# A decoder layer on eight cores: first Q tiles over six PSUM banks, earlier loads and norms of group B, LayerNorm 1 in tile order, and a rebalanced tail

## The chip, the cores and the metric

The kernel runs on all eight cores of one Trainium2 chip, as two dies of four cores (cores 0 to 3 and 4 to 7). Each core computes 2048 of the 16384 token positions. The time is the device time of the slowest core, in microseconds (us). Most executions agree within a few us (the fast ones of the kernel before took 3064.58 to 3069.06); some fall into a slower state in which one die, or both, show a lower granted TensorE clock (one of 3357.17 us had 0.90 on die 1 and 0.99 on die 0), and those are left out. Verdicts use fast executions alone, and less than 2% counts as "same".

The engines are named as the profile names them: PE is TensorE, PEld its weight loads, DVE VectorE, ACT ScalarE, POOL GpSimd, SP SyncE (which here only issues DMAs). In the lines of the profile `arena` is the one SBUF tensor that the program cuts into buffers, and `sp` its PSUM banks.

## The reference, cut to what matters

```python
D_MODEL = 2048; SEQ = 16384; D_FF = 5632
def token_mixer(x, ...):
    proj = x @ w_in + b_in
    # group A: 8 heads of 128, causal attention over three dilations (1, 4, 16), mixed
    ya = dilated_mixture_attention(qa, ka, va)
    # group B: 16 query heads of 64, 2 key/value heads, sliding window 128, with sinks
    yb = sink_window_attention(qb, kb, vb, sinks)
    y = concatenate([rms_norm(ya, g_mix_a), rms_norm(yb, g_mix_b)], -1)
    return y @ w_out
def reference(x, ...):
    x = layer_norm(ALPHA * x + token_mixer(x), ln1_g, ln1_b)      # LN1
    return layer_norm(ALPHA * x + swiglu(x), ln2_g, ln2_b)        # LN2
```

Matmuls run on bf16 operands and sum in f32.

## The kernel before: the parts that matter

A core passes through seven stages: the V projections, the first Q tiles, the attention of group B and then of group A (32 "units" each, with the remaining Q projections mixed in), the output projection (with LN1), the feed-forward part, and a tail that finishes LN2. The token block is handled in two halves of 1024, `st` = 0 and 1, from the output projection on. A helper records each operation with the buffers that it reads and writes, and the semaphores follow from that.

The first Q tiles. Each tile takes 16 matmuls into one PSUM bank, and the banks alternate between 6 and 7:

```python
def proj(tau, half=None):
    ...
    bk = 6 + tau % 2
    ...
LEAD = 6
for tau in range(LEAD):
    proj(tau)
    if tau:
        run(peq, 1)
pend = b_S(0, 0)            # first scores of group B
```

The sums for group B's RMS norm end in a small tensor, rb. It goes to DRAM from a scratch buffer `ls`, which ACT needs again in the next unit:

```python
S_.act(... out=ls, in_=ls, func=AF.Exp, scale=-0.5 ...)
S_.dma("act", k.rb_d[...], ls, [bls], [b], ...)
```

`ys` is y, the attention output, in DRAM. In unit 26 of group A SP issues the loads of rb and of 28 of the 32 pieces of y, for both halves; SP works through them in order (on core 4 these 32 issues went from 917.15 to 957.48 us, and the store of y behind them was issued at 957.58). `out_norm` multiplies one 128x512 piece of y by its norm on DVE, in place:

```python
for t in range(4):
    S_.dma("sp", k.rs[t][0], k.rb_d[...], ...)
for c in KCB:                # group B's pieces
    y_load(0, c)
for c in KCA[:6]:            # group A's pieces, without the last two heads
    y_load(0, c)
for c in KCB + KCA[:6]:
    y_load(1, c)
```

The output projection. A step takes one tile (n, hh): columns n of the model, half hh of the tokens. The tile z = ALPHA * x + projection is formed by DVE from the PSUM bank and from `xres`, a 256 KB load of x. POOL and ACT add up its statistics, and `finish` sums them over partitions with two matmuls:

```python
OUT_BK = (6, 7, 0, 1, 2, 3)
for si, (n, hh) in enumerate(steps):
    bk = OUT_BK[si % 6]
    load_xr(si + 3)                         # xres of a later tile, issued by SP
    ...
    out_mm(k, st, n, hh, bk, KCB + KCA, True, True)
    ...
    z, bz = slot("z%d_%d" % (st, si), o_h + (zbase[st] + si) * 2048)   # zbase = [12, 0]
    S_.dve(... z = ALPHA * xb + bank(k, bk) ...)
    ...                                     # statistics on ACT and POOL
    for _ in range(2 if si % 2 else 1):
        if jobs and not fins:
            jobs.pop(0)()                   # LN1 tiles of the other half
...
for hh in range(2):                         # LN1 tiles of this half become jobs
    for n in range(KC):
        jobs.append(... ln1_tile(st, n, hh, z, bz))
```

`ln1_tile` normalises z in place (two DVE operations), writes x1 in bf16 for the next matmuls and stores z to DRAM (`x1s`). Only when that store has landed is the slot of z free. The slots are tight: with `zbase` 12 and 0, z tile `si` of the second half takes the slot of z tile `si - 12` of the first. The last four tiles of the second half (`si` 28 to 31) load their xres into slots of z tiles 28 to 31 of the first half, because the ring of xres buffers has by then been given to the weights of the feed-forward part:

```python
if st == 1 and si >= 28:
    xr.append(slot("xrz%d" % si, o_h + (si + 12) * 2048))
```

The softmax here doesn't subtract the row's maximum and nothing guards it: scores larger than these inputs give would overflow.

Of the kernel before, what the change touches and what calls it, by code (L numbers as in the profile page):

```python
# [44 lines left out]
class Sched:  # L45
# [83 lines left out]
    def emit(self, final_wait_ops):  # L129
# [60 lines left out]
        for i in final_wait_ops:  # L190
            op = self.ops[i]
            last[op.semkey] = max(last.get(op.semkey, 0), op.val)
# [92 lines left out]
def persist(k):  # L285
# [14 lines left out]
    k.p_end = P.o  # L300
    for v, d in ((k.bqk, k.bqk_d), (k.bsw, k.bsw_d), (k.gmix, k.gmix_d), (k.lnp, k.lnp_d), (k.esink, k.sinks_d)):
        S_.dma("sp", v, d, [], [], "small", joins=[bs])
# [51 lines left out]
def phase1(k):  # L354
# [49 lines left out]
    o_r = XO + 4 * X_SLOT  # L404
    bvr, bbvr = view(k, o_r, VW, F32)[0:1], S_.buf("bvr", o_r, o_r + VW * 4)
    S_.dma("sp", bvr, k.bv_d[0][0:1], [], [bbvr], "bvr")
# [190 lines left out]
def phase2(k):  # L597
# [122 lines left out]
    def proj(tau, half=None):  # L720
# [10 lines left out]
        bk = 6 + tau % 2  # L731
# [236 lines left out]
    def reduce_b(t):  # L968
        bk = 6 + nx("pj", 2)
        S_.pe(lambda: nc.tensor.matmul(bank(k, bk), k.onesf, acc[:, t * 512:(t + 1) * 512], start=True, stop=True),  # L970
              [bacc[t], k.bonesf], [k.bBK[bk]])
        ls, bls = LS[nx("ls", 2)]
        S_.act(lambda: nc.scalar.activation(out=ls, in_=bank(k, bk), func=AF.Ln, bias=1024.0 * RMS_EPS, scale=1.0), [k.bBK[bk]], [bls])
        S_.act(lambda: nc.scalar.activation(out=ls, in_=ls, func=AF.Exp, scale=-0.5), [bls], [bls])
        b = Buf("rb%d" % t)
        S_.dma("act", k.rb_d[:, t * 512:(t + 1) * 512], ls, [bls], [b], "rbs%d" % t)
        rsum.append(b)

    LEAD = 6
    for tau in range(LEAD):  # L980
        proj(tau)
        if tau:
            run(peq, 1)
    pend = b_S(0, 0)
# [16 lines left out]
    for u in range(32):  # L1001
        h, c = u // 4, u % 4
        if c == 0 and h < 7:
            load_kv(h + 1)
        if u == 26:
            k.o_w, k.o_rs = o_w, o_ra
            run(dveq, 9)
            out_open(k, rsum)
        if u == 28:
            k.y_load(0, 6)  # L1010
            k.y_load(1, 6)
            wfill(k)
        for p_ in range(3):
# [11 lines left out]
            if u >= 28:  # L1025
                out_norm(k, *k.norms.pop(0))
# [8 lines left out]
    for i, (n, hh) in enumerate(OUT_PRE):  # L1035
        if i == 0:
            while len(k.norms) > 48:
                out_norm(k, *k.norms.pop(0))
# [4 lines left out]

KCB, KCA = list(range(8, 16)), list(range(8))
# [7 lines left out]
def out_open(k, rsum):  # L1052
# [16 lines left out]
    for t in range(4):  # L1069
        S_.dma("sp", k.rs[t][0], k.rb_d[:, t * 512:(t + 1) * 512], [rsum[t]], [k.rs[t][1]], "rs")  # L1070
    for c in KCB:
        y_load(0, c)
    for c in KCA[:6]:
        y_load(0, c)
    for c in KCB + KCA[:6]:
        y_load(1, c)
# [13 lines left out]
    k.wlive, k.wts = [("xr", 20480, W_RING)], {}  # L1090

# [44 lines left out]
def phase3(k):  # L1136
# [53 lines left out]
    def ln1_tile(st, n, hh, z, bz):  # L1190

        (mu, bmu), (rs, brs) = stat[hh]
        if st == 0:
            for bk, (v, b) in ((4, stat[hh][0]), (5, stat[hh][1])):
                if n == 0:
                    S_.act(lambda bk=bk, v=v: nc.scalar.activation(out=bank(k, bk), in_=v, func=AF.Copy), [b], [k.bBK[bk]])
            mu, rs, bmu, brs = bank(k, 4), bank(k, 5), k.bBK[4], k.bBK[5]
# [22 lines left out]
    for st in range(2):  # L1220
# [22 lines left out]
        for si, (n, hh) in enumerate(steps):  # L1243
            bk = OUT_BK[si % 6]
            load_xr(si + 3)
            xb, bxb = xrs[si]
            if st == 0 and si < 6:
                out_mm(k, st, n, hh, bk, KCA, False, True)
# [4 lines left out]
            for _ in range(2):  # L1253
                if st == 0 and k.norms:
# [18 lines left out]
        b0 = 4 if st == 0 else 6  # L1273
        fins += [lambda b0=b0: finish(0, b0), lambda b0=b0: finish(1, b0)]
        open_x1b(st)
        for hh in range(2):
            for n in range(KC):
# [29 lines left out]
    def finish_last(zl, bzl):  # L1307
# [18 lines left out]
        on_pool = (1, 4, 7, 10, 12, 14)  # L1326
# [15 lines left out]
        for n in range(KC):  # L1342
# [5 lines left out]
    for st in range(2):  # L1348
# [37 lines left out]
        for si, (n, hh) in enumerate(steps):  # L1386
# [34 lines left out]
            if jobs:  # L1421
                jobs.pop(0)()
# [117 lines left out]
```

## Time and profile before

| | before |
|---|---|
| fast runs, first measurement | 3064.58 and 3069.06 us |
| slow run | 3301.43 us |
| profiled execution | 3068.1 us, core 4 slowest; other cores 3050.9 to 3061.2 |

The page of the profile gives the span and the busy time of each engine (us, share of the span, number of instructions):

```profile
span 3068.1 us, 39918 instructions; the slowest of 8 cores (3050.9 to 3068.1 us)
PE 2964.0 (97%) x15721; PEld 1425.1 (46%) x15999; DVE 1057.6 (34%) x1440; ACT 656.0 (21%) x906; POOL 631.5 (21%) x593
```

PE bounds the kernel: busy 97% of the span, and 99.5% of the feed-forward part (1215 to 3034 us). PE's waits on core 4 of the kernel before (waiting line, what it waited for, us in total, times, longest):

```profile
PE sp L1130 <- DVE arena L1119: 11.2, 2, 10.7
PE sp L420 <- DMA arena<-bv: 10.3, 1, 10.3
PE sp L896 <- DVE arena L927: 8.8, 13, 3.5
...
PE sp L1130 <- DVE arena L1261: 5.8, 1, 5.8
PE sp L736 <- DVE arena L349: 3.9, 4, 1.1
PE sp L1366 <- DVE arena L1261: 3.7, 1, 3.7
PE sp L776 <- ACT arena L783: 2.2, 1, 2.2
PE sp L1366 <- DMA arena<-wup: 1.6, 1, 1.6
```

L1130 is the output projection, L1119 the norm of y, L1261 the forming of z, L736 a Q projection, L776 the first scores of B, L1366 the first feed-forward matmul ("up").

The chain of work that ended last, on core 4, shows what stands behind three of them (start, us, what):

```profile
957.58 11.89 DMA ys<-arena
969.52 3.82 DMA arena<-ys
974.11 0.76 DVE arena L1119
975.00 12.83 PE sp L1130 x48
...
1136.90 21.43 DMA x1s<-arena
1158.56 0.69 DVE arena L1261
...
1180.71 26.12 DMA x1s<-arena
1206.96 4.17 DMA arena<-xres
```

The last piece of y is stored at 957.6, read back, normalised, and only then can PE go on at 975.0. In the middle of the second half, at 1158.6, z waits for a slot whose x1s store took 21 us; at the end an xres load waits for a store of 26 us.

The timeline of PE on core 4 shows the first Q tiles and the first scores (start, us, engine, line, operation, count, idle time before and what ended it):

```profile
503.06 3.61 PE L736 MATMUL sp<-arena 128*128 128x512 bf16 x16 [0.95 <-DVE arena L349]
...
524.06 0.62 PE L776 MATMUL sp<-arena 64*128 64x256 bf16 x10 [2.18 <-ACT arena L783]
```

With two banks, each tile from the third on waits about 1 us until DVE has emptied the bank of the last but one.

### The profile page before, as it was taken

The numbers are of one execution on the slowest core, as the hardware profiler recorded it, in microseconds if no ns is written. First come the engines' busy times: TensorE is split into PE (matmuls) and PEld (weight loads), VectorE is DVE, ScalarE is ACT, GpSimd is POOL, SyncE is SP. The second block draws the span as 40 slices with busy tenths as digits, with TensorE's granted clock in tenths as the row PEclk, the third lists the DMA queues.
The fourth block names the chain that finished last, engine by engine and source line by source line (L and its number), as shares of the span: only waits on it lengthen the run. The fifth ranks groups of instructions, "written<-read, shape, count | busy, mean of one in ns | idle before, by whom it ended". The sixth has DMA issues, their size and how long they took to land.

```text
span 3068.1 us, 39918 instructions; the slowest of 8 cores (3050.9 to 3068.1 us)
## 1 busy us (share of the span) xinstructions
PE 2964.0 (97%) x15721; PEld 1425.1 (46%) x15999; DVE 1057.6 (34%) x1440; ACT 656.0 (21%) x906; POOL 631.5 (21%) x593
## 2 busy tenths in 40 slices
PE   8999999999997998999999999999999999999996
PEld 3445554545664443444444444444444444444442
DVE  1646545887787653430000100000322000000124
ACT  0000001765654133320000001111222000011123
POOL 2000000553444965000000002222000000002234
PEclk9999999999999999999999999999999999999998
DMA  9961213255657898564444348899676444435565
GB/s 165 180 142 61 87 44 75 46 124 134 134 130 192 172 185 178 130 130 77 79 73 83 69 99 205 207 205 203 140 153 135 83 76 75 81 102 178 185 206 168
DMA packets 192956, 397.92 MB, mean 130 GB/s; under 512 B 88961, under 2 KB 106625, under 8 KB 171778
## 3 DMA queue, kind: packets, MB, share of 16 engines
q0 software_dynamic: 31296, 167.06, 32.9%
q1 hardware_dynamic: 144770, 197.86, 21.9%
q10 hardware_dynamic: 16704, 30.42, 2.8%
q8 instruction: 129, 2.11, 0.3%
q14 instruction: 57, 0.47, 0.1%
HBM read 470.52 MB, written 91.82 MB: 183 GB/s over the span
## 4 chain that ended last, share of the span: by engine, by line
PE 91%; DMA 3%; ACT 2%; DVE 1%; SPq 1%; issue 1%; POOL 0%; DVEq 0%; ACTq 0%; POOLq 0%
PE sp L1366 39%; PE sp L1399 20%; PE sp L486 7%; PE sp L473 6%; PE sp L736 5%; PE sp L1130 5%; DMA x1s<-arena 2%; SPq L127 1%; PE sp L536 1%; PE sp L554 1%; PE sp L907 1%; DVE arena L927 1%; PE sp L795 1%; ACT arena L925 1%; PE sp L896 0%
## 5 line engine op out<-in xcount | busy, mean ns | idle before, releaser
L1366 PE MATMUL sp<-arena 128*128 128x512 bf16 x5519 | 1212.1, 379 | 11.2 <-DVE arena L1261 3.7
L1366 PEld LDWEIGHTS sp<-arena 128*128 128x128 bf16 x5632 | 551.3, 98 | 672.7 <-issue 10.6
L1399 PE MATMUL sp<-arena 128*128 128x512 bf16 x2760 | 605.3, 379 | 2.9
L1374 DVE TENSOR_TENSOR arena<-sp,arena 128x512 bf16<-128x512 f32 x176 | 121.8, 692 | 993.7 <-ACT arena L1373 993.7
L1399 PEld LDWEIGHTS sp<-arena 128*128 128x128 bf16 x2816 | 275.5, 98 | 332.6 <-issue 0.6
L1373 ACT ACTIVATE arena<-sp 128x512 f32<-128x512 f32 x176 | 105.1, 597 | 900.5 <-PE sp L1366 900.0
L127 POOL DMA_DIRECT2D arena<-wup x88 | 46.8, 532 | 1079.6 <-PE sp L1366 1063.1
L1170 POOL TENSOR_TENSOR arena<-arena 128x512 f32<-128x512 f32 x119 | 157.5, 1324 | 447.9 <-DVE arena L1410 393.5
L1130 PE MATMUL sp<-arena 128*128 128x512 bf16 x1003 | 225.3, 384 | 18.2 <-DVE arena L1119 11.2
L736 PE MATMUL sp<-arena 128*128 128x512 bf16 x979 | 229.9, 380 | 7.7 <-DVE arena L349 3.9
L1410 DVE SCALAR_TENSOR_TENSOR arena<-arena,sp 128x512 f32<-128x512 f32 x64 | 44.0, 688 | 520.8 <-ACT arena L1394 350.5
L486 PE MATMUL sp<-arena 128*128 128x512 bf16 x1001 | 220.1, 379 | 1.2
L473 PE MATMUL sp<-arena 128*128 128x384 bf16 (+1 forms) x1036 | 182.4, 337 | 0.4
L1130 PEld LDWEIGHTS sp<-arena 128*128 128x128 bf16 x1024 | 100.9, 99 | 143.3 <-issue 26.6
L1171 POOL TENSOR_TENSOR arena<-arena 128x512 f32<-128x512 f32 x119 | 160.3, 1347 | 1.1 <-ACT arena L1169 1.1
L486 PEld LDWEIGHTS sp<-arena 128*128 128x128 bf16 x1024 | 100.2, 98 | 120.3
L736 PEld LDWEIGHTS sp<-arena 128*128 128x128 bf16 x1024 | 96.8, 98 | 114.4 <-issue 9.2
L699 DVE TENSOR_TENSOR arena<-arena 128x1024 bf16<-128x1024 bf16 x160 | 141.3, 897 | 23.6 <-ACT arena L783 12.6
L473 PEld LDWEIGHTS sp<-arena 128*128 128x128 bf16 x1040 | 101.7, 98 | 79.6
L1394 ACT ACTIVATE arena<-arena 128x512 f32<-128x512 f32 x64 | 52.0, 813 | 394.9 <-DMA arena<-x1s 393.9
L343 ACT ACTIVATE arena<-sp,arena 128x512 bf16<-128x512 f32 (+1 forms) x37 | 25.1, 678 | 505.3 <-PE sp L510 383.1
L1169 ACT ACTIVATE arena<-arena 128x512 f32<-128x512 f32 x119 | 74.9, 630 | 201.6 <-DVE arena L1261 71.2
(130 smaller groups left out, 2062.2 us busy)
## 6 DMA issues: line engine op xcount, KB each, us to landing
arena<-wup POOLq DMA_DIRECT2D x88, 1024.0 KB, 8.2
arena<-wdb SPq DMA_DIRECT2D x32, 1408.0 KB, 7.7
arena<-wdn POOLq DMA_DIRECT2D x16, 1408.0 KB, 12.9
wdb<-arena SPq DMA_DIRECT2D x16, 1408.0 KB, 13.5
arena<-wout POOLq DMA_DIRECT2D x32, 512.0 KB, 10.7
arena<-xres SPq DMA_DIRECT2D x64, 256.0 KB, 8.6
x1s<-arena ACTq DMA_DIRECT2D x64, 256.0 KB, 8.1
arena<-x1s SPq DMA_DIRECT2D x64, 256.0 KB, 7.8
```

What stands on the lines that cost most here:

```text
L127: return self._add(q, lambda: eng.dma_start(out=out, in_=in_), reads, writes, joins, semkey=semkey)
L473: ins = nc.tensor.matmul(bank(k, bk)[:, 0:c1 - c0], x[:, kc, blk * 128:blk * 128 + 128], wv[:, kc, c0:c1], start=(kc == 0), stop=(kc == KC ...
L486: ins = nc.tensor.matmul(bank(k, bk), wk[h][:, kc, :], x[:, kc, :], start=(kc == 0), stop=(kc == KC - 1))
L699: S_.dve(lambda: nc.vector.tensor_tensor(out=pg, in0=pg, in1=m.to_broadcast([128, rows, 1024 // rows]), op=ALU.mult), [bp, b], [bp])
L736: ins = nc.tensor.matmul(bank(k, bk), w[:, kc, :], x[:, kc, :], start=(kc == 0), stop=(kc == KC - 1))
L1130: ins = nc.tensor.matmul(bank(k, bk), w[:, kc, :], y[:, kc, hh * 512:(hh + 1) * 512], start=(first and i == 0), stop=(last and i == len(kc ...
L1170: S_.pool(lambda: nc.gpsimd.tensor_tensor(out=za, in0=za, in1=z, op=ALU.add), [bz, bza], [bza])
L1171: S_.pool(lambda: nc.gpsimd.tensor_tensor(out=qa, in0=qa, in1=sq, op=ALU.add), [bsq, bqa], [bqa])
L1366: ins = nc.tensor.matmul(bank(k, a + half), w[:, kc, half * 128:half * 128 + 128], xb[:, kc, hh * 512:(hh + 1) * 512], start=(kc == 0), st ...
L1373: S_.act(lambda si=si, a=a: nc.scalar.activation(out=sg[si][0], in_=bank(k, a), func=AF.Silu), [k.bBK[a]], [sg[si][1]])
L1374: S_.dve(lambda si=si, a=a, f=f, hh=hh: nc.vector.tensor_tensor(out=h[f][:, hh * 512:(hh + 1) * 512], in0=bank(k, a + 1), in1=sg[si][0], o ...
L1399: ins = nc.tensor.matmul(bank(k, bk), w[:, fc, :], h[fc][:, hh * 512:(hh + 1) * 512], start=(fc == 0), stop=(fc == FC - 1))
```

## The change

The change means to take each of these waits away: six banks for the first Q tiles and the scores before the sixth tile; rb stored from the accumulator and not from `ls`; group B's y loaded in unit 24 and normalised in units 25 to 27, with the y of the second half moved into the output projection; the LN1 tiles in the order (n, hh) in which the slots are needed again, with mean and deviation of both halves in four banks; and the LN2 jobs of the tail dealt out anew between DVE and POOL. The core of the diff:

```diff
-        bk = 6 + tau % 2
+        bk = 6 + tau % 2 if tau >= 4 else (0, 1, 4, 5)[tau]
...
-        S_.dma("act", k.rb_d[:, t * 512:(t + 1) * 512], ls, [bls], [b], "rbs%d" % t)
+        S_.dma("act", k.rb_d[:, t * 512:(t + 1) * 512], at, [bacc[t]], [b], "rbs%d" % t)
...
     for tau in range(LEAD):
+        if tau == LEAD - 1:
+            pend = b_S(0, 0)
         proj(tau)
...
+        if u == 24:
+            k.o_w, k.o_rs = o_w, o_ra
+            out_open(k)                       # loads y of group B, first half (8 loads)
         if c == 0 and h < 7:
             load_kv(h + 1)
         if u == 26:
-            out_open(k, rsum)
+            for i in KCA[:6]:
+                k.y_load(0, i)
...
+            if u == 24 and p_ == 2:
+                rs_load(k, rsum)              # rb loads, now on ACT's queue
-            if u >= 28:
+            if (u, p_) in NORM_AT:            # 2, 3, 3 norms in units 25-27, 2 each in 28-31
                 out_norm(k, *k.norms.pop(0))
...
-            for bk, (v, b) in ((4, stat[hh][0]), (5, stat[hh][1])):
+            i = 4 + 2 * hh
+            for bk, (v, b) in ((i, stat[hh][0]), (i + 1, stat[hh][1])):
...
-            bk = OUT_BK[si % 6]
+            bk = OUT_BK[si % 6] if st == 0 else si % 4
             load_xr(si + 3)
+            if st == 0 and si < 8:
+                for c in (KCB + KCA[:7])[2 * si:2 * si + 2]:
+                    k.y_load(1, c)            # 15 loads of the second half's y
             if st == 0 and si < 6:
-                out_mm(k, st, n, hh, bk, KCA, False, True)
+                for c in KCA:
+                    out_mm(k, st, n, hh, bk, [c], False, c == 7)
...
-        for hh in range(2):
-            for n in range(KC):
+        for n in range(KC):
+            for hh in range(2):
                 jobs.append(... ln1_tile ...)
...
-        on_pool = (1, 4, 7, 10, 12, 14)
+        on_pool = (1, 4, 7, 10, 13)
...
-            if jobs:
-                jobs.pop(0)()
+            for _ in range(1 + st):
+                if jobs:
+                    jobs.pop(0)()
```

Smaller edits are cut: the bias bv is loaded first, the norms of the second half wait until step 8 of the output projection, and the last stores and their final waits come in another order.

More of the change, by code (lines that the diff above doesn't have):

```diff
@@ L189, in emit @@
         last = {}
-        for i in final_wait_ops:
+        for i in sorted(final_wait_ops):
             op = self.ops[i]
-            last[op.semkey] = max(last.get(op.semkey, 0), op.val)
+            last[op.semkey] = max(last.pop(op.semkey, 0), op.val)
         for key, val in last.items():
@@ L300, in persist @@
     k.p_end = P.o
+    o_r = XO + 4 * X_SLOT
+    k.bvr = (view(k, o_r, VW, F32)[0:1], S_.buf("bvr", o_r, o_r + VW * 4))
+    S_.dma("sp", k.bvr[0], k.bv_d[0][0:1], [], [k.bvr[1]], "bvr")
     for v, d in ((k.bqk, k.bqk_d), (k.bsw, k.bsw_d), (k.gmix, k.gmix_d), (k.lnp, k.lnp_d), (k.esink, k.sinks_d)):
@@ L402, in load_x @@
         bx[t] = bl
-    o_r = XO + 4 * X_SLOT
-    bvr, bbvr = view(k, o_r, VW, F32)[0:1], S_.buf("bvr", o_r, o_r + VW * 4)
-    S_.dma("sp", bvr, k.bv_d[0][0:1], [], [bbvr], "bvr")
+    bvr, bbvr = k.bvr
     s0 = xs[slot_of[0]]
@@ L973, in reduce_b @@
         S_.act(lambda: nc.scalar.activation(out=ls, in_=bank(k, bk), func=AF.Ln, bias=1024.0 * RMS_EPS, scale=1.0), [k.bBK[bk]], [bls])
-        S_.act(lambda: nc.scalar.activation(out=ls, in_=ls, func=AF.Exp, scale=-0.5), [bls], [bls])
+        at = acc[:, t * 512:(t + 1) * 512]
+        S_.act(lambda: nc.scalar.activation(out=at, in_=ls, func=AF.Exp, scale=-0.5), [bls], [bacc[t]])
         b = Buf("rb%d" % t)
-        S_.dma("act", k.rb_d[:, t * 512:(t + 1) * 512], ls, [bls], [b], "rbs%d" % t)
+        S_.dma("act", k.rb_d[:, t * 512:(t + 1) * 512], at, [bacc[t]], [b], "rbs%d" % t)
         rsum.append(b)
@@ L983, in phase2 @@
             run(peq, 1)
-    pend = b_S(0, 0)
     for u in range(32):
@@ L1005, in phase2 @@
         if u == 26:
-            k.o_w, k.o_rs = o_w, o_ra
             run(dveq, 9)
-            out_open(k, rsum)
+            for i in KCA[:6]:
+                k.y_load(0, i)
         if u == 28:
             k.y_load(0, 6)
-            k.y_load(1, 6)
             wfill(k)
@@ L1035, in phase2 @@
     for i, (n, hh) in enumerate(OUT_PRE):
-        if i == 0:
-            while len(k.norms) > 48:
-                out_norm(k, *k.norms.pop(0))
         out_mm(k, 0, n, hh, OUT_BK[i], KCB, True, False)
@@ L1041, in phase2 @@
             reduce_a(i + 1)
+NORM_AT = [(u, p) for u, ps in ((25, (1, 2)), (26, (0, 1, 2)), (27, (0, 1, 2)), (28, (0, 2)), (29, (0, 2)), (30, (0, 2)), (31, (0, 2)))
+           for p in ps]
 KCB, KCA = list(range(8, 16)), list(range(8))
@@ L1049, with out_open @@
 W_RING = 24576
-def out_open(k, rsum):
+def out_open(k):
     S_ = k.S
@@ L1068, in y_load @@
         S_.dma("sp", k.y[st][:, c, :], k.ys_d[c, :, st * TS:(st + 1) * TS], [k.bys[c]], k.by[st][c], "y")
-    for t in range(4):
-        S_.dma("sp", k.rs[t][0], k.rb_d[:, t * 512:(t + 1) * 512], [rsum[t]], [k.rs[t][1]], "rs")
     for c in KCB:
         y_load(0, c)
-    for c in KCA[:6]:
-        y_load(0, c)
-    for c in KCB + KCA[:6]:
-        y_load(1, c)
     k.y_load = y_load
@@ L1090, in out_open, with rs_load @@
     k.wlive, k.wts = [("xr", 20480, W_RING)], {}
+def rs_load(k, rsum):
+    for t in range(4):
+        k.S.dma("act", k.rs[t][0], k.rb_d[:, t * 512:(t + 1) * 512], [rsum[t]], [k.rs[t][1]], "rs")
 def wfill(k):
@@ L1193, in ln1_tile @@
         if st == 0:
-            for bk, (v, b) in ((4, stat[hh][0]), (5, stat[hh][1])):
+            i = 4 + 2 * hh
+            for bk, (v, b) in ((i, stat[hh][0]), (i + 1, stat[hh][1])):
                 if n == 0:
                     S_.act(lambda bk=bk, v=v: nc.scalar.activation(out=bank(k, bk), in_=v, func=AF.Copy), [b], [k.bBK[bk]])
-            mu, rs, bmu, brs = bank(k, 4), bank(k, 5), k.bBK[4], k.bBK[5]
+            mu, rs, bmu, brs = bank(k, i), bank(k, i + 1), k.bBK[i], k.bBK[i + 1]
         S_.dve(lambda: nc.vector.tensor_tensor(out=z, in0=z, in1=mu, op=ALU.subtract), [bz, bmu], [bz])
@@ L1253, in phase3 @@
             for _ in range(2):
-                if st == 0 and k.norms:
+                if st == 0 and si >= 8 and k.norms:
                     out_norm(k, *k.norms.pop(0))
@@ L1272, in phase3 @@
             jobs.pop(0)()
-        b0 = 4 if st == 0 else 6
-        fins += [lambda b0=b0: finish(0, b0), lambda b0=b0: finish(1, b0)]
+        fins += [(lambda hh=hh, b0=(4 + 2 * hh if st == 0 else 6): finish(hh, b0)) for hh in range(2)]
         open_x1b(st)
-        for hh in range(2):
-            for n in range(KC):
+        for n in range(KC):
+            for hh in range(2):
                 z, bz = zz[(n, hh)]
@@ L1341, in finish_last @@
             S_.pool(lambda z=z: nc.gpsimd.tensor_tensor(out=z, in0=z, in1=rs, op=ALU.mult), [bz, brs], [bz])
-        for n in range(KC):
+        for n in [0, 2, 1, 3, 5, 4, 6, 8, 9, 7, 11, 12, 10, 14, 15, 13]:
             ln2_out(n, TS + 512, *zr[(1, n, 1)], "sp")
```

## The prediction

> **What bounds it.** TensorE. The busy table has PE at 97% (2964 of 3068.1 us); in the windows of the feed-forward stages (1215 to 3034 us) it is 99.5%. What can be won is in about 104 us of PE idle time and in the half-rate matmuls after long idles. PE's waits (core 4) and the timeline show where:
>
> - start: 10.3 us for the DMA of bv, 0.9 for ACT;
> - first Q tiles, 495-527 us: four waits of 1 us (projection waits for DVE to empty bank 6/7), 2.2 (scores wait for exp), 0.4, then six matmuls at 0.43 instead of 0.216 us;
> - 712.8 us: 3.5 us, ACT held by the DMA store of rb from its scratch buffer;
> - 975 us: 10.65 us. The chain of waits runs through the ys store issued at 957.6 and its reload at 969.5; the store stood on the SP queue behind 28 y loads that took 35 us to issue. Then 11 matmuls at 0.43 us: 2.3 us more. [...];
> - 1153 us: 5.8 us (PSUM bank <- DVE <- a slot whose x1s store took 21 us), plus 2.3 slow;
> - 1200-1212 us: 1.6 + 3.7 us: the last out-projection tiles wait for xres behind a 26 us x1s store;
> - tail: last down matmul 3038.7, end 3068.1; POOL's sixth tile ends at 3061.4, a leftover tile is stored at 3063.7.
>
> **The change, costed.**
> 1. bv first: ACT still waits for the small loads (10.5 us) and its table load; other cores wait for wv: 1 us.
> 2. Six banks, scores before the sixth tile: 3.9 + 2.6 + 1.3 slow = 8 us, all on PE's chain.
> 3. rb stored from acc: 2-3 us.
> 4. B's y at unit 24, the second half's y moved to the out projection, rb loads on ACT's queue: removes 10.65 + 2.3 + 0.6. Adds four norms (0.75 us or more of DVE) in units 25-27, takes one each from 28-31: zero net. Per-chunk waits on 16 norms at 0.68 us cost 1-1.5. The 8 y loads (2 MB at some 200 GB/s: 10 us) delay head 7's K/V: 0-3 us risk. Net 10-12 on core 4, 6-9 on the others, whose wait was 5.6-8.4.
> 5. Tile order: the 1153 stall goes (8 us on core 4, 0-3.5 elsewhere). The end of that stage stays or gets a few us worse: DMA share is 1.0, and the first up tile now needs the banks of tiles 28 and 29, which wait for the last stores.
> 6. 15 y loads (3.9 MB) in the first out projection: DMA share of 0.3-0.6 at 980-1000 has room; 1 us lost.
> 7. Tail: POOL ends at 3057.7 with five tiles, DVE gets one more (1.2 us), no leftover: 5 us.
>
> Core 4: about 32 us. Others: about 23 from 3051-3061. The slowest core decides: 3038 us (1.0% faster), range 3024-3053. Chances: faster by over 2% 0.03, within 2% 0.96, slower 0.01.
>
> **Right or wrong will show** as: no L736/L776 waits between 495 and 527; out_mm's wait for norms under 2 us on every core; no PE gap in mid second out projection, but one of 3-8 us at its end; last store 5 us earlier relative to the last matmul; PE idle about 25 us smaller.
>
> **What would make it wrong:** late K/V of head 7 stalling PE at units 27-28; DMA saturation [...] turning xres loads into bank waits now that four banks rotate; DVE overfull at units 25-27; a slow state.

Two passages are cut from this text, where it is marked. No term of the sum was in them: it stands at about 32 us for core 4 and about 23 for the others. What the text calls slow or half rate is in the trace of core 4: behind the waits of 10.65 and 5.82 us the granted clock was 0.50 (974 to 978 us, 1158 to 1164), with one matmul every 0.427 us in place of 0.216. The table load of step 1 took ACT 1.28 us. For the 200 GB/s of step 4 the trace has 206 and 273 GB/s in the two windows of 10 us from 940, at DMA shares of 1.04 and 1.01.

## The result

The kernel after took 3058.36 us (median of four fast runs, 3054.99 to 3060.24), the kernel before 3066.03 (median of its three fast runs, 3064.58 to 3069.06; a fourth was slow). The ratio of the two is 0.9972, with a 95% interval of 0.9952 to 0.9992. A ratio here is the mean time of one kernel's fast runs over that of the other's of the same rounds, so it is not quite the ratio of the quoted medians. The class "within 2%" was right. The time was not: 3058 lies above the predicted range of 3024 to 3053, and of the 30 us that the prediction expected, 8 came.

The stages tell where. This table is worked out from the traces: from the first matmul of one stage to that of the next, in us, as the median of the eight cores of one profiled execution. There are two profiles of each kernel; the second ones are the runs a_before and a_after below.

```
                        before    before 2   after     after 2    predicted change
start to first Q         494.5     493.8     493.8     493.9      -1
first Q to end of B      205.0     205.2     196.5     196.5      -8
attention of A           250.8     251.0     251.6     251.8      -2 to -3
output projection        243.4     243.1     250.2     244.4      -6 to -20
feed-forward            1834.9    1833.5    1834.3    1833.8       -
tail                      29.2      29.1      24.8      23.7      -5
```

("First Q to end of B" ends at the first value matmul of group A, since the sixth Q tile has moved past B's first scores and that earlier mark would count it as a gain.) The first Q tiles and the tail gave what was expected. The attention of group A gave nothing, and the output projection became longer instead of shorter. In the first pair core 4, the slowest before, went from 3068.1 to 3052.9 us: 8.8 less up to the end of B, 4.3 in the tail, 2.7 in the feed-forward part and 0.3 at the start, against 0.4 more in the attention of A and 0.5 in the output projection. The slowest core is now core 7.

The page of the kernel after, core 7:

```profile
span 3059.1 us, 40208 instructions; the slowest of 8 cores (3041.8 to 3059.1 us)
PE 2987.2 (98%) x15999; PEld 1427.6 (47%) x15999; DVE 1063.9 (35%) x1442; ACT 656.1 (21%) x906; POOL 624.0 (20%) x591
```

PE's idle time went from 104 to 72 us, more than the 25 that the prediction named, and yet the profiled span fell by 9. The reason is that this trace has all 15999 matmuls and the other had not, so the two idle times cannot be compared. The waits can. PE's waits on core 7 of the kernel after:

```profile
PE sp L1375 <- DVE arena L1271: 10.2, 1, 10.2
PE sp L897 <- DVE arena L928: 9.3, 14, 2.0
PE sp L537 <- ACT arena L423: 7.3, 1, 7.3
...
PE sp L1184 <- POOL arena L1175: 3.2, 1, 3.2
PE sp L421 <- DMA arena<-bv: 2.7, 1, 2.7
PE sp L1135 <- DVE arena L1271: 2.3, 4, 0.6
PE sp L537 <- DMA arena<-wv: 2.2, 1, 2.2
...
PE sp L1135 <- DVE arena L1124: 0.6, 2, 0.3
```

L1135 is now the output projection, L1124 the norm, L1271 the forming of z, L1375 the up matmul, L1184 the statistics matmul and L1175 the POOL addition before it. The list adds up to 48.1 us. The waits that the change aimed at are gone: 11.2 for the norm is 0.6 (on all eight cores), the Q tiles and first scores wait for nothing. Three others have come in their place: 10.2 us before the first up matmul, 3.2 for POOL's statistics, and bank waits of 0.6 each. The wait for bv only changed its name: PE waits less for bv (2.7 for 10.3) and then for ACT and wv.

The first of the new waits in the trace. Busy time by engine in windows of 10 us on core 7 after (window, its length, busy us and instructions of PE, PEld, DVE, ACT, POOL, then the granted clock, the share of the DMA engines and GB/s):

```profile
950.00:960.00 10.00, 9.38 (x41) 3.83 (x40) 7.17 (x11) 1.81 (x3) 0.00 (x0) 1.00 0.01 4
960.00:970.00 10.00, 10.00 (x48) 4.41 (x46) 6.59 (x11) 2.38 (x4) 5.61 (x6) 1.00 0.41 100
970.00:980.00 10.00, 10.00 (x42) 4.21 (x41) 1.38 (x2) 1.90 (x3) 9.96 (x11) 0.85 0.98 207
980.00:990.00 10.00, 10.00 (x48) 4.56 (x47) 3.02 (x3) 0.63 (x1) 3.34 (x3) 1.00 1.04 197
```

SP issued four xres loads and the first two y loads by 945. The next xres load needs a buffer that z tile 0 frees only at 963, SP works in order, and so 13 y loads stood behind it while the DMA engines were idle (share 0.01). When SP went on, the y loads filled the engines (share 0.98 and 1.04), the next xres loads came late, and DVE had no tile to form; POOL, which adds up the statistics of those tiles, was busy 3.3 of 10 us. The waits of DVE, and those of POOL, on core 7 in that stretch (940 to 1000, and 940 to 1075):

```profile
DVE arena L1271 <- DMA arena<-xres: 22.4, 5, 9.7
```

```profile
POOL arena L1175 <- DVE arena L1271: 20.0, 9, 6.3
```

POOL has 64 such additions of about 1.27 us (1.64 to 1.72 for some of those beside norms) and cannot make up for it, so PE waits 3.17 us for the statistics at 1072. In the kernel before, POOL was no faster (L1170, the same addition, took 1.32 us on the mean of all 119, for 1.31 after), but PE stood still for 10.65 us at 975 and reached the statistics only at 1084.5. The old wait had hidden the next one.

DVE is then full from 1000 to 1050: its 26 norms take 0.74 to 3.1 us each there (mean 1.66), for 0.75 us at 953 to 963, when POOL did nothing beside them. That is a factor of 2.2 on the mean, beside POOL's additions, while the forming of z (L1271), which has one input in SBUF and one in PSUM, stays at 0.67 to 0.69 us in the same stretch. Why the norms take longer is not shown. A full DMA alone did not do it: on core 4 before, ten norms from 974.8 took 6.7 us together with POOL idle, while the DMA share was 0.94 and then 0.82 (974 to 978 us).

The second new wait, in the chain of work of core 7 after, at the end of the output projection:

```profile
1165.19 22.11 DMA x1s<-arena
1187.42 10.90 DMA arena<-xres
1199.44 15.58 PE sp L1375 x60
```

The last xres loads go into slots of z tiles 28 to 31 of the first half. In tile order these four are normalised and stored last. On this core their stores take 18 to 26 us at a DMA share of 0.94 to 1.02 (windows of 10 us from 1150 to 1190), xres comes behind, and the first up matmul, which needs banks of these tiles, starts 10.2 us late. About a dozen matmuls at half rate follow (granted clock 0.50, one every 0.427 us in place of 0.216).

In the attention, the four rb loads now stand on ACT's queue. The timeline of ACT on core 7 after:

```profile
893.22 2.15 ACTq L127 DMA_DIRECT2D arena<-rb  x4
895.47 0.60 ACT L925 ACTIVATE arena<-sp 128x512 f32<-128x512 f32 x1 [3.44 <-issue]
```

Issuing them took 2.15 us, ACT's gap grew from 1.6 (a unit earlier) to 3.4, and PE waited 1.95 us for the result at 897.7.

The first profile has one thing more. Die 1 ran 56 to 73 us of the output projection at a granted clock of 0.812 in the trace's records, called 13/16 here (one matmul every 0.263 us in place of 0.216). By the clock this costs 0.1875 of that time, an estimate of 10.6 to 13.7 us. (The traces grant it by pairs of cores: 73.1 us on cores 4 and 5, 56.4 on 6 and 7, 15.1 on 2 and 3, none on 0 and 1.) Without it core 4's stage would have been about 237 us, but the stage of core 0, which had none of it, is the longest of all (257.3). Over the 16 cores of two profiles each, with that loss taken off, the median of the stage is 241.5 us before and 243.5 after, and the longest is 249.8 before and 257.3 after. So the gain that was predicted there is missing with the clock set aside as well.

### The profile page after: what moved, and what is told of

Its sections match the earlier page's. It is cut to its first block, busy times and chain, and to the rows that moved or that the text cites. A ratio compares the mean times of both kernels' runs of the same rounds, so it can differ in the third digit from the quotient of the medians.

```text
span 3059.1 us, 40208 instructions; the slowest of 8 cores (3041.8 to 3059.1 us)
## 1 busy us (share of the span) xinstructions
PE 2987.2 (98%) x15999; PEld 1427.6 (47%) x15999; DVE 1063.9 (35%) x1442; ACT 656.1 (21%) x906; POOL 624.0 (20%) x591
## 4 chain that ended last, share of the span: by engine, by line
PE 87%; DMA 5%; DVE 3%; issue 2%; ACT 2%; POOL 1%; ACTq 0%; SPq 0%; DVEq 0%; POOLq 0%
PE sp L1375 40%; PE sp L1408 20%; PE sp L487 7%; PE sp L474 6%; PE sp L737 5%; DMA arena<-xres 3%; DMA arena<-wv 1%; PE sp L555 1%; DVE arena L1124 1%; PE sp L908 1%; DMA x1s<-arena 1%; PE sp L1135 1%; DVE arena L928 1%; PE sp L796 1%; ACT arena L926 1%
## 5 line engine op out<-in xcount | busy, mean ns | idle before, releaser
L1375 PE MATMUL sp<-arena 128*128 128x512 bf16 x5632 | 1219.0, 380 | 10.2 <-DVE arena L1271 10.2
L1375 PEld LDWEIGHTS sp<-arena 128*128 128x128 bf16 x5632 | 551.6, 98 | 678.1 <-issue 16.2
L1408 PE MATMUL sp<-arena 128*128 128x512 bf16 x2816 | 608.3, 379 | 0.0
L1175 POOL TENSOR_TENSOR arena<-arena 128x512 f32<-128x512 f32 x119 | 156.1, 1312 | 458.3 <-DVE arena L1419 404.8
L1135 PE MATMUL sp<-arena 128*128 128x512 bf16 x1024 | 233.3, 391 | 3.0 <-DVE arena L1271 2.3
L737 PE MATMUL sp<-arena 128*128 128x512 bf16 x1024 | 235.5, 379 | 0.0
L487 PE MATMUL sp<-arena 128*128 128x512 bf16 x1024 | 222.2, 379 | 0.0
L1135 PEld LDWEIGHTS sp<-arena 128*128 128x128 bf16 x1024 | 102.0, 100 | 134.9 <-issue 42.0
L487 PEld LDWEIGHTS sp<-arena 128*128 128x128 bf16 x1024 | 100.2, 98 | 120.3
L700 DVE TENSOR_TENSOR arena<-arena 128x1024 bf16<-128x1024 bf16 x160 | 144.4, 916 | 21.0 <-ACT arena L871 10.6
```

The source lines that it names most:

```text
L487: ins = nc.tensor.matmul(bank(k, bk), wk[h][:, kc, :], x[:, kc, :], start=(kc == 0), stop=(kc == KC - 1))
L700: S_.dve(lambda: nc.vector.tensor_tensor(out=pg, in0=pg, in1=m.to_broadcast([128, rows, 1024 // rows]), op=ALU.mult), [bp, b], [bp])
L737: ins = nc.tensor.matmul(bank(k, bk), w[:, kc, :], x[:, kc, :], start=(kc == 0), stop=(kc == KC - 1))
L1135: ins = nc.tensor.matmul(bank(k, bk), w[:, kc, :], y[:, kc, hh * 512:(hh + 1) * 512], start=(first and i == 0), stop=(last and i == len(kc ...
L1175: S_.pool(lambda: nc.gpsimd.tensor_tensor(out=za, in0=za, in1=z, op=ALU.add), [bz, bza], [bza])
L1375: ins = nc.tensor.matmul(bank(k, a + half), w[:, kc, half * 128:half * 128 + 128], xb[:, kc, hh * 512:(hh + 1) * 512], start=(kc == 0), st ...
```

## The experiments

All ran beside the kernel before on the same chip, on three chips labelled a, b and c. Measured against the kernel before, every run here is "same" by the 2% rule, and most of the intervals overlap; what tells the runs apart is the stages and waits of one profiled execution of each, with its eight cores. Theory one, from the traces: what the change itself put into the output projection took the gain back, in two places that have nothing to do with each other, the y loads among the xres loads (POOL, banks) and the slots of the last xres loads (first up matmul). The first rival: the lower clock seen on die 1 came with the change and made the stage long.

### a_before and a_after: the two kernels unchanged

There is no edit. They give a second profile of each, and show whether the clock belongs to the change.

> The kernel before, unchanged, for a second profile on the same chip as the runs beside it. If the clock of 13/16 that the trace of the changed kernel shows in the out projection (some 56 us of it on core 7) belongs to the chip or the die, it appears here as long, and the second die has a lower clock than the first. If it comes with the change (PE no longer pausing in the out projection), it is under 20 us per core here. Stage from first out-projection matmul to first up matmul: 238 to 250 us per core.

> The changed kernel, unchanged, for a second profile. Stage from first out-projection to first up matmul 242 to 257 us per core, of which 3 to 11 us are the wait of the first up matmul on most cores; if the 13/16 clock is tied to the change it is again there, 40 to 60 us per core on one die at least.

Measured: a_before 3062.02 us, a_after 3059.74 (3059.32 and 3060.17), ratio 0.9993 with an interval of 0.9969 to 1.0018. Here the kernel before had 14 to 15 us at 13/16 in the output projection, on six cores, and the kernel after 10 to 17 us on die 0 alone. The new waits were there with and without it: 3 us for POOL on seven of the eight cores, 2.6 to 10.8 us before the first up matmul. Under 20 us in a_before alone would have spoken for the rival, but the changed kernel had no more here and its waits all the same. The rival falls.

### a_slots: the last xres loads in slots that are stored earlier

```diff
-                    xr.append(slot("xrz%d" % si, o_h + (si + 12) * 2048))
+                    xr.append(slot("xrz%d" % si, o_h + (si + 4) * 2048))
```

These are the slots of z tiles 20 to 23 of the first half.

> The changed kernel with one number changed: the residual loads of the last four out-projection tiles land in the slots of first-half tiles 20 to 23, normalised and stored some 8 steps before the loads, in place of tiles 28 to 31, stored 2 to 4 steps before. Theory one (the loads stand behind the stores of the last normalised tiles): the wait of the first up matmul falls from up to 11 us to under 1.5 us on every core, with it 2 to 5 us of half-rate matmuls, and the time by 5 to 12 us on the slowest core. Theory two (the DMA engines are simply full and the loads late in any case): the wait stays over 3 us on most cores.

Measured: 3051.37 and 3055.41 us (two more runs were slow), ratio 0.9973 [0.9949, 0.9997]. The wait for DVE before the first up matmul is gone on all eight cores, and the stage's median is 241.7 us. PE's waits on core 7 in the output projection, in this run:

```profile
PE sp L1135 <- DVE arena L1271: 6.4, 8, 2.3
...
PE sp L1184 <- POOL arena L1175: 3.2, 1, 3.2
```

The wait for POOL and the bank waits stayed, as theory one says. The last four stores took 18 to 36 us here, no less than in a_after (8 to 30), so it is the slots and not the time of the stores that made the difference. Core 6 now waited 8.1 us for weights.

### a_yearly: all y loads of the second half before the first step

```diff
-        for si in range(3):
+        for si in range(4):
             load_xr(si)
+        if st == 0:
+            for c in KCB + KCA[:7]:
+                k.y_load(1, c)
         for si, (n, hh) in enumerate(steps):
             bk = OUT_BK[si % 6] if st == 0 else si % 4
-            load_xr(si + 3)
+            if si:
+                load_xr(si + 3)
             xb, bxb = xrs[si]
-            if st == 0 and si < 8:
-                for c in (KCB + KCA[:7])[2 * si:2 * si + 2]:
-                    k.y_load(1, c)
```

The same 15 loads are issued without a stop into the gap in which the DMA engines were idle.

> The changed kernel with the 15 loads of the second half's y issued before the first out-projection step (DMA idle there from 945 to 960 us) in place of two per step between the residual loads. Theory one (y between the residual loads starves the tiles, so POOL's statistics are late): DVE's wait for residuals at 965 to 1000 us falls from 22 us to under 8, the statistics' matmul no longer waits for POOL (3.2 us to under 1, and 1.7 us of half rate gone): 3 to 5 us less in the stage. Theory two (POOL alone is too slow, 64 operations of 1.27 us): the wait for POOL stays at 2 us or more.

Measured: 3047.28, 3052.38 and 3054.23 us, ratio 0.9961 [0.9937, 0.9985]. PE's waits on core 7 in the output projection, in this run (lines are one higher than after):

```profile
PE sp L1376 <- DVE arena L1272: 8.1, 1, 8.1
...
PE sp L1135 <- DVE arena L1272: 1.4, 2, 0.9
```

The wait for POOL is gone on all cores, the bank waits are 0 to 1.4 us, and DVE's wait for xres up to 1000 us fell from 22.4 to 4.2 us on core 7. The wait before the first up matmul stayed (2.9 to 13.7 us). The stage's median is 235.6 us. So the two causes are separate, each follows its own edit, and moving the 15 loads was worth 9 us of the stage against a_after, where 3 to 5 were expected. All of it lies before the first statistics matmul: every core took 120.1 to 120.4 us up to there, for 122.4 to 134.4 in a_after. (The total fell less on cores 2 and 3, which lost 11 us to a lower clock before the first Q tile, and on cores 0 and 1, which lost 8 to 12 in the feed-forward part.)

### b_both: both edits together

The edit is the two diffs above on the kernel after.

> The changed kernel with both edits: early loads of the second half's y, and the last residual loads into slots stored long before. If the two waits were all that took the gain back, neither wait is left on any core (statistics for POOL under 1 us, first up matmul under 1.5 us), the stage from first out-projection to first up matmul is 228 to 235 us on cores without the 13/16 clock (242 to 257 in the changed kernel), and the time is 15 to 25 us under that of the kernel before, some 3040 us. If the DMA engines are the true limit of the stage, a new wait (weights, residuals, banks) of some 5 us or more turns up in their place.

Measured: 3044.71 us (median of three fast runs, 3042.01 to 3046.33; a fourth was slow), ratio 0.9923 [0.9894, 0.9952]. The output projection's median is 232.3 us and three cores have about 227, which is what the matmuls alone take (1024 of 0.2157 us make 221, and the statistics matmuls come on top). The limit that remains is a new one, on half the cores: PE's waits on core 4 in the output projection, in this run:

```profile
PE sp L1376 <- DMA arena<-wup: 6.4, 1, 6.4
PE sp L1135 <- DVE arena L1272: 2.4, 2, 1.8
```

The first up matmul now waits for its weights.

### b_both_norms: group B's norms back in units 28 to 31

```diff
+        if i == 0:
+            while len(k.norms) > 48:
+                out_norm(k, *k.norms.pop(0))
...
-NORM_AT = [(u, p) for u, ps in ((25, (1, 2)), (26, (0, 1, 2)), ...) for p in ps]
+NORM_AT = [(u, p) for u in range(28, 32) for p in range(3)]
```

This is on b_both. It asks whether DVE's norms in units 25 to 27 cost the attention its gain.

> The same, with group B's norms back where the kernel before had them (three per unit from unit 28, the last four after the attention). Theory: norms in units 25 to 27, where DVE also does the last rope, hold PE in the attention; then PE's waits in its last 130 us fall from 13-14 us to under 12 and the half-rate periods of 3 to 10 us there go: 1 to 3 us gained. Rival: the norms are only moved and units 28 to 31 lose what 25 to 27 gain: no difference over 1 us.

Measured: 3045.11 us (median of four, 3043.15 to 3047.32), ratio 0.9926 [0.9907, 0.9946], so the same as b_both. The attention of A has a median of 252.6 us against 251.7. The theory that the early norms cost something falls; but they gained nothing either.

### b_hhorder: LN1 back in the old order, with two statistics banks

```diff
-            i = 4 + 2 * hh
+            i = 4
...
-            bk = OUT_BK[si % 6] if st == 0 else si % 4
+            bk = OUT_BK[si % 6]
...
-        for n in range(KC):
-            for hh in range(2):
+        for hh in range(2):
+            for n in range(KC):
```

This is on the kernel after (the bank of `finish` goes back with it).

> The changed kernel with the tile order of LN1 and its four statistics banks undone. Theory: the tile order only traded a wait in the middle of the second out projection for one at its end. Then bank waits in the middle come back (2 to 6 us on about half of the cores), the first up matmul's wait falls under 4 us, and the stage is as long as in the changed kernel within 3 us. Rival (the tile order is a gain that other things hide): the stage is 5 us or more longer on most cores.

Measured: 3054.15 and 3057.76 us, ratio 0.9962 [0.9933, 0.999]. PE's waits on core 1, the worst, in the output projection:

```profile
PE sp L1135 <- DVE arena L1271: 16.2, 8, 6.8
PE sp L1375 <- DMA arena<-wup: 1.9, 1, 1.9
```

The first up matmul waits at most 3.3 us for DVE (core 7) and 4.1 for weights, and the stage's median is 241.3 us, not longer than with tile order. So far the theory holds. The bank waits are 7.6 to 16.2 us on five cores, but they are not where it put them: the wait in the middle of the second half came back on core 1 alone (3.7 us). The others lie in the first half, which this edit does not touch, and before the first matmul of the second half (0.6 to 6.8 us on seven cores), where the old order of banks takes bank 6 again two tiles after its last use. So tile order and four banks gained nothing as they stood, and that tile order took away the mid-stage wait of the kernel before is not shown.

### b_sure: the kernel before with the six banks and the new tail alone

The edit is the hunks of the diff for `proj`, `LEAD`, `on_pool` and the tail, on the kernel before.

> The kernel before with only the first Q tiles over six banks and the tail's jobs rebalanced. Both are on PE's chain at places that nothing follows up: the first score starts 8 us earlier after the first Q matmul (18 in place of 26 us), the tail after the last matmul is 24 in place of 29 us, everything between is as in the kernel before, and the time is 12 to 14 us lower (0.4%). If the out projection takes gains back whatever comes before it (its loads bound it), the 8 us of the Q tiles are not seen at the first up matmul.

Measured: 3053.3 us (median of four, 3048.77 to 3056.11), ratio 0.9951 [0.9932, 0.9971]. First Q to the end of B takes 196.5 us and the tail 24.1, as after, and the output projection is unchanged at 244.0. The attention of A takes 249.4 us, 2.2 less than after, and PE's waits in its last 130 us or so add up to 10.1 to 11.4 us against 12.5 to 13.8 after. PE's wait at the first unit of A is 2.0 us on six cores here (2.0 to 4.2 before, 1.9 on all after), though rb is still stored from `ls`. All the rest of the change, rb and y and LN1, was therefore no gain, and perhaps a small loss: 0.9951 without it, 0.9972 and 0.9993 with it, with intervals that overlap.

### c_rs: the rb loads issued by POOL

```diff
-        k.S.dma("act", k.rs[t][0], k.rb_d[:, t * 512:(t + 1) * 512], [rsum[t]], [k.rs[t][1]], "rs")
+        k.S.dma("pool", k.rs[t][0], k.rb_d[:, t * 512:(t + 1) * 512], [rsum[t]], [k.rs[t][1]], "rs")
```

This is on the kernel after.

> The changed kernel with one word changed: the four loads of rb in unit 24 are issued by POOL in place of ACT. Theory: issuing them takes ACT 2.2 to 2.7 us between the last scores and the logarithm of unit 24, more than the 1.6 us it has there; then PE's wait at the start of unit 25 (1.95 us) falls to the 0.4 us of other units, and the span from the first score to the first out-projection matmul, 428 to 431 us, falls by 1.5 to 3 us, to the 427 us of the run with only the Q tiles and the tail. Rival (the y loads ahead of head 7's keys and values, or the norms, are what costs): under 0.7 us of change.

Measured: 3055.57 us (median of four, 3051.74 to 3057.03), ratio 0.9969 [0.9947, 0.9992]. The issue time moved as it should. The timeline of POOL on core 7 in this run:

```profile
890.61 2.19 POOL L127 DMA_DIRECT2D arena<-rb  x4 [2.33 <-DVE arena L331]
```

The wait of 1.95 us at 897.7 went with it, but on core 7 another of 2.8 us came at 903.3, where a norm waited for rb itself. The attention of A has a median of 251.4 us for 251.6, where the theory asked for 1.5 to 3 us less: the gain did not come. The other issuing engine only moved the time of the issue: 2.15 us were taken off ACT, 2.19 put on POOL, and the loads took no less time: the first landed 9.8 us after its issue, for 8.0 in the kernel after.

### c_best: b_both with c_rs

> Early y loads, slots stored long before, and the rb loads issued by POOL: the candidate for the best version. Some 2 us less than the run of the first two edits, ratio to the kernel before about 0.991 to 0.992.

Measured: the fast runs took 3038.87 and 3040.01 us, ratio 0.9921 [0.9892, 0.9949]; four of six runs, among them the profiled one, were slow. In the profile die 1 has a mean clock of 0.97, from some 350 us at 13/16 in the V projections (cores 4 and 5) or the feed-forward part (6 and 7). On die 0, which had 31 to 35 us of it, all in the output projection, that stage took 232.8 to 234.0 us with no wait but the 0.6 for the norms and 0.9 for weights on one core; on die 1 core 6 waited 5.0 us for weights and the others at most 0.7.

### c_best2: b_both with the loads in another order

```diff
+        if c == 0 and h < 7:
+            load_kv(h + 1)
         if u == 24:
             k.o_w, k.o_rs = o_w, o_ra
             out_open(k)
-        if c == 0 and h < 7:
-            load_kv(h + 1)
...
-        k.S.dma("act", k.rs[t][0], ...)
+        k.S.dma("sp", k.rs[t][0], ...)
```

This is on b_both_norms. In unit 24 the last head's keys and values come first, then y; rb follows on SP's queue, for which the late norms leave time.

> Early y loads, slots stored long before, head 7's keys and values loaded ahead of group B's y, rb on the SP queue behind them, norms from unit 28 on. If late keys and values were what costs in the attention, the span from first score to first out-projection matmul is 2 us or more under that of the candidate beside it; if the rb loads on ACT were it, the two are the same within 1 us.

Measured: 3038.47 us (median of four fast runs, 3035.13 to 3042.16; a fifth was slow), ratio 0.9918 [0.9898, 0.9937]. It is correct and faster than both kernels, though still within the 2%. The page of this run:

```profile
span 3038.6 us, 40212 instructions; the slowest of 8 cores (3021.6 to 3038.6 us)
```

The attention of A has a median of 249.8 us, 1.9 less than with b_both and 1.8 less than in the profile of c_best on the same chip. The edit took away two things at once, the delay of the keys and values and the issue of rb on ACT, and so it does not say which of them gave the 1.9 us.

### c_half: half of xres

```diff
-                S_.dma("sp", xrs[si][0], k.xres_d[n, :, c0:c0 + 512], [], [xrs[si][1]], "xr")
+                w_ = 512 if st == 0 else 256
+                S_.dma("sp", xrs[si][0][:, 0:w_], k.xres_d[n, :, c0:c0 + w_], [], [xrs[si][1]], "xr")
```

This is on b_both. The second half loads only half of each xres tile, so the result is wrong (relative error 0.63). It asks whether the waits that b_both has left, for weights and banks, come from the number of bytes or from the order in which POOL issues the weights.

> Wrong result on purpose: early y loads and slots as before, but the residual loads of the second out projection bring 256 of 512 columns (4 MB of some 23 MB less through the DMA engines). Two cores of eight still waited 6 to 7 us there for the first up weights. If the DMA engines' throughput is the limit on those cores, such waits and the bank waits go on all cores (each under 1 us, stage 227 to 229 us); if the order of issue on POOL's queue is, waits of 3 us or more stay on two or more cores.

Measured: 3037.97 us in one run. All waits for banks and weights in the output projection are gone on all eight cores. Of PE's waits on core 7 in that stretch, one line belongs to the output projection:

```profile
PE sp L1135 <- DVE arena L1124: 0.6, 2, 0.3
```

The stage takes 227.4 us on the two cores that had no 13/16 clock, and 231.6 to 233.9 on the six that had 25 to 37 us of it: 36.6 us times 0.1875 is 6.9, and 233.9 less 227.4 is 6.5. This fits the bytes that the DMA engines have to move as the limit there, with the issues in the same order, but one run does not show it. PE was slower on six of the cores, which may have given the loads more time (the author's reading, not shown apart), and c_best, which moves all the bytes, left waits over 1 us on one core only. The two cores at full clock are too few: of the cores at full clock in b_both and b_both_norms, with all the bytes, 6 of 16 had no such wait over 1 us either.

### The output projection in all runs

The median and range over the eight cores, in us, worked out from the traces. The last two numbers cut the stage in two at the first statistics matmul, two tiles into the second half; they are medians with the loss to the 13/16 clock taken off, so they do not add up to the first.

```
               median   range            first part  rest    waits left
before         243.4   238.0 to 249.8    129.1      113.3    norm 6-11, bank, weights, first up matmul
a_before       243.1   237.6 to 249.8    129.5      111.0    as before
after          250.2   242.0 to 257.3    128.6      113.6    POOL, bank, first up matmul
a_after        244.4   236.7 to 257.4    129.2      115.1    as after
a_slots        241.7   233.2 to 253.6    130.8      108.8    POOL, bank, weights
a_yearly       235.6   231.8 to 242.3    120.3      114.0    first up matmul
b_both         232.3   227.2 to 239.5    120.4      112.1    weights, bank (up to 7)
b_both_norms   231.6   227.2 to 238.5    120.3      111.3    weights, bank (up to 8)
b_hhorder      241.3   233.7 to 252.8    133.1      109.9    bank, POOL, weights
b_sure         244.0   238.5 to 246.9    129.7      114.1    as before
c_rs           244.3   235.5 to 252.7    129.5      109.8    as after
c_best (slow)  232.6   227.4 to 234.0    120.3      107.0    weights on one core
c_best2        233.3   227.4 to 239.6    120.4      109.4    weights, bank (up to 6)
c_half         232.1   227.4 to 233.9    120.3      106.8    none; clock of 13/16
```

The first part falls by 9 us exactly where the y loads come early, and on every core. The rest is less clear: it spreads by up to 18 us between the cores of one execution, and a slower PE may give the loads more time: in c_best the cores of die 0, with 31 to 35 us at 13/16, waited 0.9 us at most, and cores at full clock in b_both up to 7. No run separates the two. No run has the early loads and LN1 in the old order together, so what tile order is worth with both repairs stays untested.

## Why the prediction was right or wrong

- **What bounds it: right, with one number misread.** PE bounds the kernel, and its waits were read in the right places. The figure of 104 us of idle time was too high, since 278 matmul records were missing; the waits of that core add up to 61.6 us.
- **Start (step 1): about right, 0 to 1 us for 1.** PE no longer waits long for bv, but for ACT and wv instead.
- **First Q tiles (step 2): right.** Up to the end of B, 205 us became 196.5, on every core of every run with the edit.
- **rb from the accumulator (step 3): mis-sized.** The wait at the first unit of group A was 2.0 to 4.2 us on the cores before and 1.9 after: on core 4 it fell by 1.5 us, for the 2-3 us counted. Most of the drop comes without this edit as well (b_sure), with the earlier timing that the Q tiles bring.
- **Early y and norms (step 4): its wait fell, its gain did not come.** The wait for the norm fell to 0.6 us on all cores, as named. "zero net" for the attention was wrong by about 2 us (b_sure against after), and the cause of these is not shown. The issue of four rb loads on ACT took 2.15 us, which the step did not count, but taking it off ACT did not shorten the attention (c_rs). The feared delay of the keys and values showed as no wait in the profile after, and how much the order of loads cost is open (c_best2). Moving the norms of units 25 to 27 back gained nothing (b_both_norms).
- **Tile order (step 5): the mid-stage wait went, perhaps by luck, and the end was mis-sized.** The wait was gone on six of eight cores, but without tile order it stayed away as well (b_hhorder), so the reason given for it is not shown. "stays or gets a few us worse" and "3-8 us at its end" was 0 to 11.3 us, and half-rate matmuls behind it. a_slots shows the cause: the four slots that are stored last. The "8 us on core 4, 0-3.5 elsewhere" did not come: even with the slots repaired the rest of the stage took 112.1 us (b_both), for 114.1 without the step on the same chip (b_sure).
- **15 y loads (step 6): this is the step that failed most.** "has room; 1 us lost" was read from the DMA share before. The loads did not meet that idle time: they stood behind an xres load that waited for a buffer, and then came all at once in front of the xres loads. It cost 3.2 us on POOL, bank waits of up to 11 us and half-rate matmuls. a_yearly shows it: the same 15 loads, issued in the idle time, made the stage 9 us shorter than a_after's and took away the wait for POOL. So the step's 1 us was 9, and that is as much as step 4 had won in the first part of the stage: 129.5 us before and 129.2 after, 120.3 with early loads, all on one chip.
- **Steps 4 to 6 together:** predicted 6 to 20 us shorter, measured 2 us longer at the median with the clock set aside. The sum took each wait that the change removed as gained. In that stage POOL's statistics (PE waits 3.17 us for them at 1072), DVE (busy all of 1000 to 1050) and the DMA engines (share 0.98 and 1.04 from 970 to 990, all on core 7 after) were close behind PE, and the old waits had covered them. With both repairs the stage became 11 us shorter than before (b_both), within the range predicted for it, 9 of them in its first part.
- **Tail (step 7): right.** 29.2 us became 24.8 and 23.7.
- **What would make it wrong:** "turning xres loads into bank waits" was named, and it came, but mostly not "now that four banks rotate": that is in the second half, and most of these waits were in the first, where six banks rotate. It was given too little weight: the range should have held the case in which this stage gives nothing.

Four things stay open: which of the two reorderings in c_best2 gave 1.9 us, what took away the mid-stage wait, what limits the rest of the stage when both repairs are in, and what decides when a pair of cores gets the 13/16 clock. The last differed by chip and run and not by kernel (in the output projection none on the second chip in four kernels; on the third 15 to 37 us in all four, on four or six of the eight cores).

## What to carry to other kernels

When a wait is removed, ask what else reaches the same point next, and when: here POOL, which was done in time behind a stall of 10.65 us, was 3.17 us late without it. The free DMA time (share 0.01 from 950 to 960) was of no use to 13 loads that stood on SP behind an xres load without a buffer, and the same 15 loads issued ahead of it made the stage 9 us shorter (a_yearly), so look for what the queue waits on before putting loads behind it. And when buffers change their order of release, follow every later user of those slots, the last ones first.

## What the traces show of clock, issues, transfers and norms

- In the fast runs all eight cores ran dense matmuls for about 1834 us of feed-forward, at a mean granted clock of 1.00 in the two cores looked at (windows of cores 4 before and 7 after), and 13/16 came in pieces, 0 to 73 us of the output projection and at most 70 us of the feed-forward part (core 0 of a_yearly); on one chip (b) the output projection had none in the profiles of four kernels. In some slow runs it lasted: one of a_slots had die 0 at a mean of 0.81 for 3632 us, with die 1 at 0.99 beside it.
- The issue of a load held its engine for 0.33 us (xres, SP), 0.53 (wup, POOL) or 0.57 (wout and wdn, POOL) at the median, and the load landed after 8 to 13 us (core 7 after). For an issuing engine that also computes the time counts: four loads held ACT 2.15 us and POOL 2.19 us, as long as three or four of ACT's own operations of 0.6 us.
- The 256 KB stores of x1s landed in 8 us at the median, and those issued from 1114 to 1152 us in 28 to 33 us, at a DMA share of 0.96 (core 7 after).
- A norm with one bf16 and one f32 input of 128x512 in SBUF took 0.75 us beside an idle POOL and 0.74 to 3.1 us, 1.66 on the mean, beside its f32 additions of 1.26 to 1.72 us (core 7 after, 953 to 963 and 1000 to 1050 us).
